# Dilated attention's merge: factors spread through DRAM, the sum of two groups on GpSimd, output weights loaded earlier

## The chip, the cores and the metric

The kernel runs on one core of a Trainium2 chip. The metric is the device time of one execution in microseconds (us); where several runs are given, their median stands for the kernel. The engines of a core run side by side, each in its own order: TensorE (PE; PEld is its weight load), VectorE (DVE), ScalarE (ACT), GpSimd (POOL), and SyncE (SP), which issues nearly all DMAs here. All arithmetic is in 32-bit floats. TensorE multiplies in a rounded 32-bit format (`F32R`), so every operand is split into a high and a low part, and a product is three matmuls (hi x hi, hi x lo, lo x hi).

## The reference

A trunk of two layers over 1024 positions of width 1024. Layer 0 is a gated MLP mixer, layer 1 dilated attention; each is followed by a dense MLP. The change lies in layer 1:

```python
for g, (window, dil) in enumerate(((128, 1), (512, 4), (2048, 16))):
    n_, d_, m_ = _dilated_group(...)     # numerator, denominator, row maximum of this group
...
m_all = jnp.max(jnp.stack(maxs), axis=0)
scales = [jnp.exp(m_ - m_all) for m_ in maxs]
num_sum = sum(n_ * c[..., None] for n_, c in zip(nums, scales))
den_sum = sum(d_ * c for d_, c in zip(dens, scales))
o = (num_sum / den_sum[..., None]).astype(h.dtype).reshape(B_, S_, ATT_WIDTH)
return o @ w_out
```

Each of 8 heads of width 64 attends in three groups of its own keys (dilations 1, 4 and 16). For each position and head the three results are added with three factors, which depend on the groups' maxima and denominators alone.

## The kernel before

Activations lie with features on the partitions and positions along the row. The attention stage works on 4 pairs of heads (`hp`), each pair in three units (`g` in the order 1, 2, 0), so 12 units. The main loop `unit_qkv(i)` computes the queries and keys of unit `i`, two products `m` of 48 matmuls of 128x512; the last unit has a third product for its values. While PE works on them, `attention()` fits in the scores, softmax and values of the unit before, in four steps `j`.

The order of PE's instructions is written out by a planner, `Flow`. It holds a clock that every matmul advances by an estimate. Side jobs are Python generators that yield a time after which they may go on (many from the table `LAT`, in ns), or an event and a time. Between the main loop's matmuls the planner lets those that are due put out their next instructions (`pump`); where the main loop has to wait for an event, `until` moves the clock to the next due side job. The other engines and SP's queue are ordered by a scheduler of the framework, by program order with a preference for what is marked `high_priority`, and as soon as operands and buffers are there. So loads are issued as far ahead as buffers allow.

The buffers that matter: `wpool`, tag "w", 8 tiles of 128x1024; a weight from `weight()` takes two of them (high and low part), loaded through 4 raw tiles (tag "r") and split at L208 (ScalarE, high part) and L209 (VectorE, low part). `at_bank()` gives one of 5 PSUM banks, `temp()` one of 8 tiles of 128x512.

`merge(hp, i)` (L1234) joins the three groups of one pair for one half `i` of the positions; there are 8 such calls. It begins when the last group's scores of that half are put out. It first forms the factors, `f`, with positions on the partitions: 128 x 3 groups x 4 blocks x 2 heads (L1242 to L1256). They are needed with features on the partitions. So for each group `factors(g)` copies the factors to 64 columns per head (L1262, ScalarE, 128x512) and `spread_factors` transposes the four 128x128 blocks into a PSUM bank (L187, PE). Then the group's numerator `N`, permuted back to the order of positions, is multiplied by it (L1279, VectorE); groups 1 and 2 are added up (L1283), and group 0's numerator is multiplied in place and gets that sum (L1290, L1291). `split_N` splits the result into the tiles `o`. For pairs 0 and 1 `project_side` follows, eight projections of `o` with the output weights `wbo` (`mm<-o`, three matmuls each, added to `h` at L306); pair 2's and 3's projections stand at the end of the stage. The next pair's values wait, in the plan, for the event `merged[hp, 1]`.

Other DMAs on SP's queue in this stage: the exchange of softmax statistics through DRAM (`sc<-st`, `ex<-sc`, L1223 to L1229), the bias tiles (`t<-bvec`, L906 and L911, copied by VectorE at L916) and the values (`V<-vd`).

Of the kernel before, what the change touches and what calls it, by code (L numbers as in the profile page):

```python
# [10 lines left out]
F32 = mybir.dt.float32  # L11
# [96 lines left out]

LAT = dict(sum=2600.0, rms=2600.0, tile=1600.0, gate=8500.0, soft=4200.0, turn=3800.0, fe=1300.0, v=2000.0, qk=2700.0, merge=2600.0, out=700.0, fex=3.0, ve=1600.0, vd=6000.0)


@with_exitstack
def trunk(ctx: ExitStack, tc: tile.TileContext, xT, w_u, w_v, w_o, w_s, b_s, w_qkv, w_vt, w_bo, rel,
# [910 lines left out]
    def unit_qkv(i):  # L1024
# [42 lines left out]
        if i < NU - 1:  # L1067
            flow.add(v_load(i))
        for m in range(3 if i == NU - 1 else 2):
            w = load(m)  # L1070
            if i == NU - 1 and m:
                proj_load(m + 1)
            both(w, KCOLS, ys, lambda s, b: out(m, s, b))
# [160 lines left out]
    def merge(hp, i):  # L1234
# [8 lines left out]
        nc.vector.tensor_tensor(mn, mn, e[2][:, :, :, 0], op=ALU.min)  # L1243
        f = small.tile([P, 3, 4, 2], F32, tag="f", name="f", bufs=2)
        for g in range(3):
            nc.vector.tensor_tensor(f[:, g], mn, e[g][:, :, :, 0], op=ALU.subtract)
        nc.scalar.activation(f, f, AF.Exp)
        dn = small.tile([P, 4, 2], F32, tag="dn", name="dn", bufs=2)
# [17 lines left out]
        def spread_factors(fe):  # L1266
            pb = at_bank()
            for b in range(4):
                transpose(pb[:, blk(b)], fe[:, blk(b)])
            return pb  # L1270

        rest = None
        fe_ns = LAT["fe"] * (2.2 if hp == 3 else LAT["fex"])
        for g in (1, 2):
            fe = factors(g)
            yield fe_ns
            pb = spread_factors(fe)
            t = temp()
            nc.vector.tensor_tensor(own(t, g), permuted(us_[g].N, i, g), own(pb, g), op=ALU.mult)  # L1279
            if rest is None:  # L1280
                rest = t
            else:
                nc.vector.tensor_tensor(rest, rest, t, op=ALU.add)  # L1283
        fe = factors(0)
        yield fe_ns
        yield valued[hp, i], 0
        N = us_[0].N[:, half(i)]
        pb = spread_factors(fe)
        with tc.high_priority(offset=PRIO):
# [39 lines left out]
    def project_side(hp, i):  # L1329
        for m in range(8 - LEFT * ((hp, i) == (1, 1))):  # L1330
            project(hp, i, m)
            yield 900
        projected[hp, i].t = flow.t
# [128 lines left out]
```

## Time and profile before

| What | Value |
|---|---|
| time before, median of 3 runs | 2188.39 us (2188.21 to 2189.08) |
| the profiled execution | 2188.09 us, span 2186.4 us |
| mean granted TensorE clock | 0.995 |
| PE, DVE, ACT, POOL busy | 2142.4, 1551.1, 1087.4, 515.5 us |
| attention stage with its merges | about 1085 to 1545 us of the span |

A row of a group reads: line, engine, operation, out<-in by tile names, shapes, count, then busy us and mean ns of one, then idle time of the engine just before and what ended it. A row of the timeline reads: start, length, engine, line, operation, count. A row of the stretches reads: stretch, length, busy us (and instructions) of PE, PEld, DVE, ACT, POOL, then clock, DMA share and GB/s. A row of the waits reads: who waited, for whom, us in total, times, longest.

### The profile page before, as it was taken

The page shows a single profiled execution, that of the slowest core. Times are in us where ns is not written, and L with a number is a line of the kernel's source. Part 1 is how long each engine was busy: PE and PEld are TensorE (multiplying, and loading weights), DVE is VectorE, ACT ScalarE, POOL GpSimd, SP SyncE. Part 2 cuts the span into 40 slices and gives each one's busy share as a digit, 9 for nine tenths or more (in the row PEclk, how much of TensorE's full clock was granted, in tenths as well). Part 3 has the DMA queues.
Part 4 walks back from the last instruction along what each step waited for, and adds up shares of the span by engine and source line. Part 5 has one row for each costly group of instructions (what it writes and reads, how often), then busy time and mean ns, then how long its engine had stood idle before and what let it go on. Part 6 is the DMA issues. An engine that isn't in the chain of part 4 may idle for free.

```text
span 2186.4 us, 30394 instructions
## 1 busy us (share of the span) xinstructions
PE 2142.4 (98%) x10360; PEld 1776.8 (81%) x10360; DVE 1551.1 (71%) x2855; ACT 1087.4 (50%) x2200; POOL 515.5 (24%) x372
## 2 busy tenths in 40 slices
PE   8999999999999999999999999999999999999997
PEld 7888887888878888788888887887778888788886
DVE  7875268766689887771357676658986667988867
ACT  7644135555564444351355564656555556544433
POOL 2000124333323333510000000001443332332335
PEclk9999999999999999999999999999999999999999
DMA  6321104444355443333322222221154443644422
GB/s 222 110 75 49 48 22 150 165 150 152 132 172 172 151 155 117 109 113 138 121 68 62 74 65 54 75 55 30 39 179 157 149 152 121 195 161 150 150 90 99
DMA packets 167679, 253.88 MB, mean 116 GB/s; under 512 B 33641, under 2 KB 59364, under 8 KB 167524
## 3 DMA queue, kind: packets, MB, share of 16 engines
q1 hardware_dynamic: 166768, 250.71, 35.7%
q8 instruction: 81, 1.33, 0.3%
q10 hardware_dynamic: 756, 1.23, 0.2%
q14 instruction: 74, 0.61, 0.1%
HBM read 182.50 MB, written 69.37 MB: 115 GB/s over the span
## 4 chain that ended last, share of the span: by engine, by line
PE 77%; DVE 10%; DMA 6%; ACT 4%; issue 2%; POOL 1%; SPq 1%; DVEq 0%; ACTq 0%; POOLq 0%
PE at L180 38%; PE mm L180 37%; PE at L187 1%; DVE wp L209 1%; ACT t L1107 1%; DMA t<-bvec 1%; DMA h<-in_xT 1%; DMA t<-hid 1%; DMA t<-in_w_dl 1%; DVE y L209 1%; DMA sc<-st 1%; DVE h L797 1%; DVE N L1145 1%; DMA hr<-hid 1%; DVE hx L209 1%
## 5 line engine op out<-in xcount | busy, mean ns | idle before, releaser
L208 ACT ACTIVATE wp<-r 128x512 fp32r<-128x512 f32 (+2 forms) x404 | 240.6, 600 | 359.1 <-PE at L180 240.3
L180 PE MATMUL at<-hx,wp 128*128 128x512 f32 x1770 | 413.1, 389 | 3.7 <-DVE h L797 3.7
L180 PE MATMUL mm<-y,whi 128*128 128x512 f32 x1312 | 412.3, 395 | 0.0
L180 PEld LDWEIGHTS at<-hx,wp 128*128 128x128 f32 x1770 | 332.0, 188 | 73.8 <-DVE h L797 4.5
L209 DVE TENSOR_TENSOR wp<-r,wp 128x512 fp32r<-128x512 f32 (+2 forms) x404 | 319.9, 801 | 66.0 <-ACT wp L208 62.3
L180 PE MATMUL at<-t,wp 128*128 128x512 f32 x1344 | 313.9, 389 | 0.1
L180 PEld LDWEIGHTS at<-t,wp 128*128 128x128 f32 x1344 | 252.2, 188 | 52.8 <-DVE t L713 0.5
L262 POOL TENSOR_TENSOR t<-t 128x512 f32<-128x512 f32 (+1 forms) x66 | 82.8, 1255 | 866.2 <-ACT t L257 864.1
L180 PEld LDWEIGHTS mm<-y,whi 128*128 128x128 f32 x1312 | 240.7, 188 | 50.6
L180 PE MATMUL mm<-y,wlo 128*128 128x512 f32 x656 | 255.9, 390 | 0.0
L180 PE MATMUL mm<-y,wp 128*128 128x512 f32 x912 | 224.3, 392 | 5.3 <-ACT t L694 4.8
L349 POOL TENSOR_TENSOR t<-r 128x512 f32<-128x512 f32 (+3 forms) x62 | 90.4, 1457 | 579.4 <-DMA r<-in_w_dn 164.2
L180 PEld LDWEIGHTS mm<-y,wp 128*128 128x128 f32 x912 | 171.5, 189 | 43.4 <-ACT t L694 5.7
L180 PE MATMUL mm<-hx,wp 128*128 128x512 f32 x708 | 172.4, 390 | 2.5 <-DVE hx L209 1.3
L180 PEld LDWEIGHTS mm<-hx,wp 128*128 128x128 f32 x708 | 132.6, 188 | 31.5 <-DVE hx L209 2.3
L209 DVE TENSOR_TENSOR hx<-t,hx 128x512 fp32r<-128x512 f32 x192 | 146.6, 770 | 1.8 <-ACT hx L208 1.8
L180 PEld LDWEIGHTS mm<-y,wlo 128*128 128x128 f32 x656 | 123.1, 188 | 26.6
L797 DVE TENSOR_TENSOR h<-h,at 128x512 f32<-128x512 f32 x144 | 97.6, 682 | 48.2 <-PE at L180 46.4
L209 DVE TENSOR_TENSOR wlo<-r,whi 128x512 fp32r<-128x512 f32 x138 | 97.6, 725 | 46.4 <-ACT whi L208 42.0
L208 ACT ACTIVATE hx<-t 128x512 fp32r<-128x512 f32 x192 | 119.0, 630 | 18.1 <-DMA t<-hid 11.7
L208 ACT ACTIVATE whi<-r 128x512 fp32r<-128x512 f32 x138 | 84.0, 627 | 88.3 <-PE mm L180 56.9
L180 PE MATMUL at<-y,wp 128*128 128x512 f32 x480 | 119.0, 390 | 0.7 <-DVE wp L209 0.7
(199 smaller groups left out, 3214.0 us busy)
## 6 DMA issues: line engine op xcount, KB each, us to landing
t<-hid SPq DMA_DIRECT2D x182, 256.0 KB, 3.5
hid<-t SPq DMA_DIRECT2D x140, 256.0 KB, 2.3
r<-in_w_up SPq DMA_DIRECT2D x128, 256.0 KB, 2.7
r<-in_w_dn SPq DMA_DIRECT2D x88, 256.0 KB, 2.6
hid<-b SPq DMA_DIRECT2D x56, 256.0 KB, 2.1
r<-in_w_qkv SPq DMA_DIRECT2D x50, 256.0 KB, 2.6
r<-in_w_v SPq DMA_DIRECT2D x48, 256.0 KB, 3.5
vd<-vs SPq DMA_DIRECT2D x16, 512.0 KB, 3.9
```

What stands on the lines that cost most here:

```text
L180: nc.tensor.matmul(out, lhsT, rhs, **kw)
L187: nc.tensor.transpose(out, src, ident)
L208: nc.scalar.activation(hi, src, AF.Copy)
L209: nc.vector.tensor_tensor(lo, src, hi.bitcast(F32), op=ALU.subtract)
L262: nc.gpsimd.tensor_tensor(self.acc, self.acc, sq, op=ALU.add)
L349: tt(r3, r[0, 0], r[1, 0], op=ALU.subtract)
L797: engine.tensor_tensor(hs[i, s], hs[i, s], src, op=ALU.add)
L1107: nc.scalar.activation(p[:, c], p[:, c], AF.Exp, bias=m, scale=-1.0, accum_out=dn)
L1145: nc.vector.tensor_tensor(o, o, pv[r, c], op=ALU.add)
```

## The change

For pairs 0, 1 and 2 the factors no longer go through ScalarE and PE. `f` is laid out so that its 24 columns (group, head, block) lie together. One transpose turns them into 24 rows of 128 (L187), VectorE copies these out of PSUM, and one DMA stores them in DRAM as 3 x 2 rows of 512 positions. Six DMAs read them back, each row to 64 partitions, into two tiles of `wpool`'s tag "w". All this is put out at once, after which the planner waits 11 us. The products of groups 1 and 2 and their sum are done by GpSimd, from SBUF; group 0's product stays on VectorE and reads SBUF instead of PSUM. Pair 3's two merges are as before. `proj_load(0)` and `proj_load(1)`, the output weights of pairs 0 and 1, are put out at the start of the first unit of the next pair instead of at the first projection. The planner leaves 1400 ns between two projections at the side, where it left 900.

```diff
@@ -106,7 +106,7 @@
 WARM = 11
 MMB = 3
 
-LAT = dict(sum=2600.0, rms=2600.0, tile=1600.0, gate=8500.0, soft=4200.0, turn=3800.0, fe=1300.0, v=2000.0, qk=2700.0, merge=2600.0, out=700.0, fex=3.0, ve=1600.0, vd=6000.0)
+LAT = dict(sum=2600.0, rms=2600.0, tile=1600.0, gate=8500.0, soft=4200.0, turn=3800.0, fe=1300.0, v=2000.0, qk=2700.0, merge=2600.0, out=700.0, sent=11000.0, proj=1400.0, ve=1600.0, vd=6000.0)
 
 
 @with_exitstack
@@ -1066,6 +1066,8 @@
 
         if i < NU - 1:
             flow.add(v_load(i))
+        if g == ORDER[0] and 0 < u.hp < 3:
+            proj_load(u.hp - 1)
         for m in range(3 if i == NU - 1 else 2):
             w = load(m)
             if i == NU - 1 and m:
@@ -1241,10 +1243,11 @@
         mn = small.tile([P, 4, 2], F32, tag="mn", name="mn", bufs=2)
         nc.vector.tensor_tensor(mn, e[0][:, :, :, 0], e[1][:, :, :, 0], op=ALU.min)
         nc.vector.tensor_tensor(mn, mn, e[2][:, :, :, 0], op=ALU.min)
-        f = small.tile([P, 3, 4, 2], F32, tag="f", name="f", bufs=2)
+        flat = small.tile([P, 3, 2, 4], F32, tag="f", name="f", bufs=2)
+        f = flat.rearrange("p g a b -> p g b a")
         for g in range(3):
             nc.vector.tensor_tensor(f[:, g], mn, e[g][:, :, :, 0], op=ALU.subtract)
-        nc.scalar.activation(f, f, AF.Exp)
+        nc.scalar.activation(flat, flat, AF.Exp)
         dn = small.tile([P, 4, 2], F32, tag="dn", name="dn", bufs=2)
         d2 = small.tile([P, 4, 2], F32, tag="d2", name="d2", bufs=2)
         nc.vector.tensor_tensor(dn, f[:, 0], e[0][:, :, :, 1], op=ALU.mult)
@@ -1269,23 +1272,49 @@
                 transpose(pb[:, blk(b)], fe[:, blk(b)])
             return pb
 
+        def sent():
+
+            pt = at_bank()
+            transpose(pt[0:24, 0:P], flat.rearrange("p g a b -> p (g a b)"))
+            ft = temp()[0:24, 0:P]
+            fd = dram.tile([3, 2, HALF], F32, tag="fd", name="fd")
+            with tc.high_priority(offset=PRIO):
+                nc.vector.tensor_copy(ft, pt[0:24, 0:P])
+                nc.sync.dma_start(fd.rearrange("g a (b p) -> (g a b) p", p=P), ft)
+            out = {}
+            place = [wpool.tile([P, 2, HALF], F32, tag="w", name="fe") for _ in range(2)]
+            for g in (1, 2, 0):
+                out[g] = place[g == 0][:, g // 2]
+                with tc.high_priority(offset=PRIO):
+                    for a in range(2):
+                        nc.sync.dma_start(out[g][64 * a:64 * a + 64], fd[g, a].partition_broadcast(64))
+            return out
+
         rest = None
-        fe_ns = LAT["fe"] * (2.2 if hp == 3 else LAT["fex"])
+        fe_ns = LAT["fe"] * 2.2
+        if hp < 3:
+            by_dma = sent()
+            yield LAT["sent"]
         for g in (1, 2):
-            fe = factors(g)
-            yield fe_ns
-            pb = spread_factors(fe)
+            if hp < 3:
+                pb = by_dma[g]
+            else:
+                fe = factors(g)
+                yield fe_ns
+                pb = spread_factors(fe)
             t = temp()
-            nc.vector.tensor_tensor(own(t, g), permuted(us_[g].N, i, g), own(pb, g), op=ALU.mult)
+            engine = nc.vector if hp == 3 else nc.gpsimd
+            engine.tensor_tensor(own(t, g), permuted(us_[g].N, i, g), own(pb, g), op=ALU.mult)
             if rest is None:
                 rest = t
             else:
-                nc.vector.tensor_tensor(rest, rest, t, op=ALU.add)
-        fe = factors(0)
-        yield fe_ns
+                engine.tensor_tensor(rest, rest, t, op=ALU.add)
+        if hp == 3:
+            fe = factors(0)
+            yield fe_ns
         yield valued[hp, i], 0
         N = us_[0].N[:, half(i)]
-        pb = spread_factors(fe)
+        pb = by_dma[0] if hp < 3 else spread_factors(fe)
         with tc.high_priority(offset=PRIO):
             nc.vector.tensor_tensor(N, N, pb, op=ALU.mult)
             nc.vector.tensor_tensor(N, N, rest, op=ALU.add)
@@ -1329,7 +1358,7 @@
     def project_side(hp, i):
         for m in range(8 - LEFT * ((hp, i) == (1, 1))):
             project(hp, i, m)
-            yield 900
+            yield LAT['proj']
         projected[hp, i].t = flow.t
 
     all_values()
```

## The prediction

> **What bounds the kernel now.** I read the page's busy times first, then one table of stretches over the attention stage (1085 to 1475 us), then the waits of that stage.
>
> ```profile
> span 2186.4 us, 30394 instructions
> PE 2142.4 (98%) x10360; PEld 1776.8 (81%) x10360; DVE 1551.1 (71%) x2855; ACT 1087.4 (50%) x2200; POOL 515.5 (24%) x372
> PE 77%; DVE 10%; DMA 6%; ACT 4%; issue 2%; POOL 1%; SPq 1%; DVEq 0%; ACTq 0%; POOLq 0%
> ```
>
> TensorE is busy for 98% of the span and carries 77% of the chain that ended last. The change lies in the attention stage only, so I look there. Columns: stretch, length, then busy us of PE, PEld, DVE, ACT, POOL.
>
> ```profile
> 1085.00:1162.00 77.00, 76.52 (x461) 62.72 (x460) 40.43 (x140) 42.42 (x131) 0.00 (x0) 1.00 0.26 69
> 1162.00:1182.00 20.00, 20.00 (x137) 17.39 (x136) 16.36 (x57) 15.23 (x40) 0.00 (x0) 1.00 0.25 80
> 1182.00:1277.00 95.00, 93.21 (x549) 76.86 (x548) 63.12 (x178) 49.57 (x145) 0.00 (x0) 1.00 0.23 63
> 1277.00:1297.00 20.00, 20.00 (x137) 17.40 (x136) 16.12 (x54) 14.42 (x37) 0.00 (x0) 1.00 0.25 79
> 1297.00:1390.00 93.00, 91.07 (x536) 74.32 (x535) 58.31 (x168) 47.13 (x140) 0.00 (x0) 1.00 0.23 59
> 1390.00:1411.00 21.00, 21.00 (x141) 18.21 (x140) 17.28 (x59) 16.21 (x42) 0.00 (x0) 1.00 0.24 77
> 1411.00:1475.00 64.00, 63.05 (x395) 52.71 (x393) 40.48 (x122) 37.65 (x112) 0.00 (x0) 1.00 0.23 56
> ```
>
> In these 390 us PE stands for 0.48 + 1.79 + 1.93 + 0.95 = 5.15 us in all. GpSimd does nothing. The three 20 us stretches are where the first merges of pairs 0, 1 and 2 begin: VectorE is at 16.4 of 20 us there, the only other engine near its limit. So PE work taken out here is time saved, as long as nothing new makes PE stand; at most 5.15 us of standing can be won on top.
>
> **What is removed.** Each of the six merges of pairs 0 to 2 (three pairs, two halves) spreads its factors three times, each time by one ScalarE copy (L1262) and four transposes (L187). Two of these spreads between matmuls:
>
> ```profile
> 1173.34 0.60 PE L187 MATMUL at<-ident,t 128*128 128x128 f32 x4
> ...
> 1186.27 0.66 PE L187 MATMUL at<-ident,t 128*128 128x128 f32 x4
> 1186.68 0.70 PE L180 MATMUL mm<-y,whi 128*128 128x512 f32 x2
> ...
> 1188.14 0.60 PE L187 MATMUL at<-ident,t 128*128 128x128 f32 x4
> 1188.50 0.71 PE L180 MATMUL mm<-y,whi 128*128 128x512 f32 x2
> ```
>
> Start to start, four transposes push the next matmul by 1186.68 - 1186.27 = 0.41 us, or 0.36. Eighteen spreads by 0.41 are 7.4 us of PE (6.5 by the other). Each merge adds one transpose, 0.10 us, so 0.6 comes back: 6.8 us net, 5.9 at the low end.
>
> ```profile
> DVE b L916 <- DMA t<-bvec: 26.2, 10, 4.6
> PE at L187 <- ACT t L1262: 0.6, 2, 0.3
> ```
>
> With the copies goes the 0.6 us that PE waited for them. Sum so far -7.4.
>
> VectorE and ScalarE are relieved too:
>
> ```profile
> L262 POOL TENSOR_TENSOR t<-t 128x512 f32<-128x512 f32 x54 | 74.0, 1371 | 860.4 <-ACT t L257 858.9
> L1279 DVE TENSOR_TENSOR t<-N,at 128x512 f32<-128x512 f32 x16 | 17.4, 1085 | 0.0
> L1262 ACT ACTIVATE t<-f 128x512 f32<-128x512 f32 x24 | 14.8, 621 | 3.2 <-DVE t L1283 3.2
> L1290 DVE TENSOR_TENSOR N<-N,at 128x512 f32<-128x512 f32 x8 | 5.5, 683 | 0.5 <-PE at L187 0.5
> L1283 DVE TENSOR_TENSOR t<-t 128x512 f32<-128x512 f32 x8 | 5.3, 668 | 0.1
> ```
>
> Per merge VectorE loses two products of 1.085 and one sum of 0.668, 2.84 us; ScalarE 3 x 0.621 = 1.86 us. Neither bounds the stage, so I book nothing for that; the bound on the gain side is the rest of PE's standing, 5.15 - 0.6 = 4.5 us. VectorE's new copy out of PSUM has 24 partitions; the 128-partition L1290 at 0.68 us bounds it from above, and VectorE's relief covers it.
>
> **What is added: the way of the factors.** I follow merge (0, 0). The planner placed group 1's old transposes 3.9 us after the factors were issued, so the new single transpose stands near 1173.34 - 3.9 = 1169.4. Then copy, store, and six loads on SP.
>
> ```profile
> hid<-t SPq DMA_DIRECT2D x140, 256.0 KB, 2.3
> t<-bvec SPq DMA_DIRECT2D x8, 256.0 KB, 4.1
> t<-bvec SPq DMA_DIRECT2D x8, 32.0 KB, 2.8
> sc<-st SPq DMA_DIRECT2D x8, 8.0 KB, 4.0
> ```
>
> A store lands in 2.3 us (wide rows) to 4.0 (16-byte pieces). The factors' rows are 512 bytes, so I take 2.3; either way, with at most 0.7 for the copy and 0.6 for an issue (below), the loads could go by 1169.4 + 0.7 + 0.6 + 4.0 = 1174.7. But they write into two tiles of the "w" pool, which has eight and which the weights fill as soon as a pair comes free:
>
> ```profile
> 1162.31 0.62 ACT L208 ACTIVATE whi<-r 128x512 fp32r<-128x512 f32 x1
> ...
> 1181.90 0.64 ACT L208 ACTIVATE whi<-r 128x512 fp32r<-128x512 f32 x1 [0.16 <-PE mm L180]
> ```
>
> Each row is a weight's split that starts when PE has done with an older weight (the second row says so). The pair that comes free at 1162.31 goes to a weight, since the factors are not there yet; the next at 1181.90. So the store is hidden, and the loads start at 1181.90.
>
> ```profile
> 1183.40 1.26 SPq L911 DMA_DIRECT2D t<-bvec  x2
> ```
>
> Two issues take 1.26 us, so group 1 lands at 1181.90 + 1.26 + 2.8 = 1186.0 (4.1 instead of 2.8 at the upper end), group 2 at 1187.2. On GpSimd no strided product is in the trace. Lower bound: L262's plain 1.37 us. Upper: the same product on VectorE takes 1.085 against 0.683 for a plain one, a factor of 1.59, which makes 2.18 us. I take 2.18, since L1279 has the same operands. So 1188.2, 1190.4, and with a sum of 1.37 1191.7. What follows is as before:
>
> ```profile
> 1189.77 0.69 DVE L1291 TENSOR_TENSOR N<-N,t 128x512 f32<-128x512 f32 x1
> 1190.50 0.64 ACT L208 ACTIVATE o<-N 128x512 fp32r<-128x512 f32 x1
> 1191.72 0.69 DVE L209 TENSOR_TENSOR o<-N,o 128x512 fp32r<-128x512 f32 x1
> 1193.86 0.70 PE L180 MATMUL mm<-o,whi 128*128 128x512 f32 x2
> ```
>
> Last sum, split: 1191.7 + 0.69 + 0.64 + 0.69 = 1193.7. Two spreads fewer before the release bring all of it forward by 0.8, to 1192.9. The planned first projection was at 1193.86; four spreads fewer ahead of it bring it to 1192.2. PE would stand 0.7 us. Lower bound 0 (with 1.37 the chain is 1.6 shorter); upper, with 4.1 per load, 2.0. Pairs 0 and 1 have this; pair 2 is projected only at the end, and second halves find the first half's tiles free and have to wait for its projection in any case. So 2 x 0.7 = 1.4 us, ends 0 and 4.0.
>
> The Trainium skill has a price for such a load in "DMA: Bandwidth & Descriptors", section "Anatomy of one DMA — SWDGE (gpsimd) path": about 2.0 us plus the bytes at 436 GB/s, for DMAs that GpSimd issues. As an estimate, 128 KB would land in 2.3 us, 0.5 sooner than the row that I used; by it the term would be 0.4 and the sum 1.0 us lower.
>
> **What is queued behind the new waits.** SP: behind the six loads stands the next bias tile (1183.40), 6 x 0.63 = 3.8 us later; its taker is VectorE's copy L916, which stands in VectorE's order. VectorE also stands at the products and sums of N until load and GpSimd are done. What such standing costs can be read off: VectorE stood 26.2 us for bias loads in 10 waits (2.6 each), and PE's standing apart from the copies was 4.5 us in all, so at most 0.17 us of PE per us of VectorE. Six merges at 2.6 are 15.7 us, at most 2.7 of PE; lower end 0. I take the middle, 1.3.
>
> **Output weights ahead.** Their loads, four DMAs and four splits for pairs 0 and 1, move past a unit's two weight loads on SP.
>
> ```profile
> 1117.04 0.89 SPq L169 DMA_DIRECT2D r<-in_w_bo  x2
> ```
>
> They are issued 77 us before first use already, being hoisted. Moved further they hold a pair of tiles longer, and two weights are split one step of the pool later (1181.90 - 1162.31 = 19.6 us). The pool's four pairs hold three weights beside the one that PE reads, so two steps of lead are left. Zero, covered by that lead; without it a first half's split, 0.64 + 0.69 us (the rows of o above), would stand ahead of each weight. **The projection's spacing** (900 to 1400 ns in the plan) costs zero too: PE has qkv matmuls to run between projections. Where it has none left, the planner moves its clock to the next due step, and the projections come back to back.
>
> **Sum.** -6.8 - 0.6 + 1.3 + 1.4 = -4.7 us. The profiled execution took 2188.1 us (span 2186.4 and 1.7 around it), the median of the runs is 2188.4. Forecast 2183.7. What a measurement of this kernel can tell from no change is about 0.2%, 4.4 us: faster begins under 2184.0.
>
> **Rivals.** (a) All of the way is hidden: pools and GpSimd idle, nothing stands; -7.4, 2181.0. For: GpSimd is free, ScalarE and PSUM banks are relieved. Against: tiles are claimed the moment they come free. (b) The freed PE time returns at the first projections and behind VectorE, both terms at their upper ends: -7.4 + 4.0 + 2.7 = -0.7, 2187.7, no change. For: the row of 1181.90. Against: it needs 4.1 us loads.
>
> (c) Slower: GpSimd's reads hold up VectorE, which then holds PE. GpSimd works 2 x 2.18 + 1.37 = 5.7 us per merge; if VectorE's work stood for all of it, it would lose 5.7 - 2.84 = 2.9 us per merge, six merges 17.2 us, all on PE where VectorE is the later one: -7.4 + 17.2 = +9.8, 2198. It turns slower once PE loses (7.4 + 4.4) / 6 = 2.0 us per merge.
>
> ```profile
> L209 DVE TENSOR_TENSOR wp<-r,wp 128x512 fp32r<-128x512 f32 x344 | 288.3, 848 | 61.1 <-ACT wp L208 57.6
> L209 DVE TENSOR_TENSOR wlo<-r,whi 128x512 fp32r<-128x512 f32 x138 | 97.6, 725 | 46.4 <-ACT whi L208 42.0
> ```
>
> For: the same subtraction takes 848 ns in the stage where GpSimd works and 725 where it mostly does not. Against: that is 17%, not a stop, and VectorE has 3.6 us of 20 free. The Trainium skill, "GPSIMD Engine Reference", section "1. Specifications", says that GpSimd shares its SBUF interfaces with VectorE, in contention with instructions that have two SBUF inputs. By that rule, taken as a full stop, this rival holds; the trace agrees in sign, with the 17%.
>
> **How the numbers follow.** Forecast 0.42, own range 2181.5 to 2186, three quarters of it (0.32) under 2184.0; (a) 0.20; (b) 0.16; (c) 0.22. Faster 0.32 + 0.20 = 0.52, same 0.10 + 0.16 = 0.26, slower 0.22. The range goes from 2179, (a) with 2 us of PE's other standing won, to 2195, which takes in (b) and the lower part of (c).
>
> **What would show it.** Right: about 66 fewer L187 transposes, PE busy some 7 us less, the first projections of pairs 0 and 1 waiting under 1 us for o, factor loads that start when a weight's matmuls end. (a): loads starting 3 us after the transpose. (b): PE standing 2 us at those projections. (c): VectorE's two-input rows stretched, and PE waiting for VectorE at scores and q, k. Wrong altogether: weights split too late for their matmuls, which I priced at nothing.

## The result, and the profile after

The changed kernel takes 2200.98 us (median of six runs, 2196.49 to 2202.48); the kernel before took 2188.73 in six runs beside it (2187.60 to 2190.91). The ratio is 1.0053, 95% interval 1.0040 to 1.0066: 12.3 us slower. The forecast of 2183.7 has the wrong sign, and the time lies above the range.

The profiled execution is the quickest of the six, 2196.49 us. Its page, two of the rows that the prediction showed of before:

```profile
span 2194.6 us, 30326 instructions
PE 2140.8 (98%) x10294; PEld 1770.3 (81%) x10294; DVE 1549.0 (71%) x2843; ACT 1078.0 (49%) x2182; POOL 545.7 (25%) x390
```

PE has 66 instructions fewer, as forecast (10360 to 10294), but only 1.6 us less busy time, and the span is 8.2 us longer. The table of stretches, with the prediction's borders (busy us of PE, PEld, DVE, ACT, POOL, then the clock):

```profile
1085.00:1162.00 77.00, 76.88 (x469) 63.65 (x467) 39.63 (x142) 42.40 (x132) 0.00 (x0) 1.00 0.24 63
1162.00:1182.00 20.00, 19.80 (x128) 16.62 (x127) 15.64 (x42) 11.22 (x31) 4.48 (x3) 1.00 0.37 120
1182.00:1277.00 95.00, 88.78 (x512) 71.48 (x513) 59.09 (x167) 46.37 (x135) 5.08 (x4) 1.00 0.27 71
1277.00:1297.00 20.00, 20.00 (x130) 17.10 (x129) 15.84 (x59) 13.12 (x37) 0.18 (x1) 1.00 0.25 73
1297.00:1390.00 93.00, 88.72 (x510) 71.42 (x510) 57.28 (x164) 45.13 (x133) 9.31 (x6) 1.00 0.30 78
1390.00:1411.00 21.00, 21.00 (x141) 17.91 (x140) 16.46 (x57) 14.14 (x40) 0.05 (x1) 1.00 0.22 68
1411.00:1475.00 64.00, 60.11 (x349) 48.85 (x348) 42.18 (x121) 35.76 (x102) 9.17 (x6) 0.97 0.32 92
```

In these 390 us PE stood 5.15 us before; now it stands 14.7. Before, the clock was 1.00 in every stretch; now the last shows 0.97. Whom PE waits for, from 1110 to 1500 us (total, times, longest):

```profile
PE at L187 <- DVE f L1259: 4.7, 3, 1.9
PE at L187 <- ACT t L1109: 3.5, 13, 0.6
PE at L180 <- DVE tr L209: 2.4, 5, 0.9
PE mm L180 <- DVE h L306: 1.9, 4, 0.8
```

The first row is new: the single transpose of the factors waits for VectorE's last product L1259 (L1256 before). The others are VectorE's and ScalarE's usual products arriving late; the second was 2.3 us before (row in the section on why the prediction was wrong).

For comparing runs I use one measure below. The **stage** goes from the first exchange store (`sc<-st`) to the last pair of them: 1110.7 to 1473.6 us before, 362.9 us; 371.4 us after, 8.45 longer. Summed from start to start over PE's instructions, transposes (L187) take 7.2 us less than before (40.7 to 33.5), so the term for the removed work had its size. But the same 1038 matmuls `mm` take 10.7 us more (246.8 to 257.5) and the 252 value products (128x128) 3.0 more: that is where waits and half clock sit.

The half clock shows only in narrow stretches. Here are two neighbouring ones of the changed kernel, and then, in the same view for L187 alone (busy us of PE and PEld), the transposes' part of the first:

```profile
1442.34:1445.76 3.42, 2.52 (x19) 1.65 (x20) 1.88 (x9) 3.31 (x12) 0.00 (x0) 1.00 0.00 1
1445.76:1449.17 3.41, 3.41 (x9) 2.63 (x9) 3.11 (x11) 2.80 (x9) 0.00 (x0) 0.50 0.51 150
```

```profile
1442.34:1445.76 3.42, 1.48 (x6) 0.68 (x6) 1.00 0.00 1
```

In the first, PE is busy for 2.52 of 3.42 us, but 1.48 of that are transposes; matmuls take 1.04 us, 30%. In the next the granted clock is 0.50, which costs up to half of 3.41 us. Before had none between 1085 and 1500 us. The granted clock of whole runs points the same way: the ten runs of before in one session had 0.9948 in the mean, the five of the changed kernel beside them 0.9912. As (1 - clock) x time that is 11.4 against 19.4 us, so up to 8 us of the 12.3 are clock ("up to", since part of it lies over waits).

### The profile page after: what moved, and what is told of

The parts are those of the page before. It is cut to its first block, busy times and chain, and to the rows that moved or that the text cites. A ratio compares the mean times of both kernels' runs of the same rounds, so it can differ in the third digit from the quotient of the medians.

```text
span 2194.6 us, 30326 instructions
## 1 busy us (share of the span) xinstructions
PE 2140.8 (98%) x10294; PEld 1770.3 (81%) x10294; DVE 1549.0 (71%) x2843; ACT 1078.0 (49%) x2182; POOL 545.7 (25%) x390
## 4 chain that ended last, share of the span: by engine, by line
PE 78%; DVE 10%; DMA 4%; ACT 4%; issue 2%; POOL 1%; SPq 1%; DVEq 0%; ACTq 0%; POOLq 0%
PE at L180 40%; PE mm L180 37%; DVE wp L209 1%; ACT t L1109 1%; PE at L187 1%; DMA fe<-fd 1%; DMA sc<-st 1%; DMA t<-bvec 1%; DVE y L209 1%; DVE h L306 1%; DVE hx L209 1%; DVE N L1147 1%; DVE h L797 1%; SPq L1290 0%; DVE t L209 0%
## 5 line engine op out<-in xcount | busy, mean ns | idle before, releaser
L208 ACT ACTIVATE wp<-r 128x512 fp32r<-128x512 f32 (+2 forms) x404 | 241.0, 600 | 366.6 <-PE at L180 247.4
L1307 POOL TENSOR_TENSOR t<-N,fe 128x512 f32<-128x512 f32 x12 | 20.5, 1732 | 464.4 <-PE at L180 426.1
L208 ACT ACTIVATE whi<-r 128x512 fp32r<-128x512 f32 x138 | 83.3, 625 | 97.0 <-PE mm L180 56.5
L208 ACT ACTIVATE hx<-t 128x512 fp32r<-128x512 f32 x192 | 118.8, 630 | 14.3 <-DMA t<-hid 10.1
```

Of the source, the lines that this page charges most:

```text
L208: nc.scalar.activation(hi, src, AF.Copy)
L1307: engine.tensor_tensor(own(t, g), permuted(us_[g].N, i, g), own(pb, g), op=ALU.mult)
```

## The experiments

All times are medians of five rounds against the kernel before on the same chip. "Stage" is the change against before's 362.9 us, "stands" what PE stands in it (pauses over 0.15 us), "half clock" half the time at 0.50 in it, all from the profiled run.

| Kernel | us | ratio to before, 95% interval | stage | stands | half clock |
|---|---|---|---|---|---|
| before | 2186.8 to 2188.7 | | 0 | 4.9 | 0 |
| c1_changed_again | 2200.99 | 1.0053 [1.0039, 1.0066] | +13.3 | 14.4 | 6.8 |
| e1_vector_sum | 2196.18 | 1.0045 [1.0032, 1.0059] | +8.6 | 11.7 | 6.8 |
| e2_later_transpose | 2211.24 | 1.0110 [1.0096, 1.0124] | +21.9 | 18.1 | 15.4 |
| e3_plan_only | 2191.57 | 1.0017 [1.0008, 1.0026] | 0.0 | 4.8 | 0 |
| e4_temps | 2211.40 | 1.0110 [1.0096, 1.0123] | +22.4 | 24.5 | 10.2 |
| g1_same_plan_vector | 2195.89 | 1.0040 [1.0027, 1.0054] | +6.7 | 14.1 | 3.4 |
| g2_same_plan_pool | 2196.36 | 1.0039 [1.0027, 1.0050] | +6.1 | 13.0 | 3.4 |
| g3_spacing_back | 2200.23 | 1.0054 [1.0042, 1.0066] | +9.2 | 15.3 | 6.8 |
| h1_hold | 2188.81 | 1.0005 [0.9996, 1.0014] | -2.1 | 4.9 | 0 |
| h2_hold_one | 2190.72 | 1.0011 [1.0002, 1.0020] | +0.8 | 6.8 | 0 |
| h3_own_tiles | 2249.27 | 1.0277 [1.0263, 1.0291] | +10.7 | 15.2 | 6.8 |
| h3c_fewer_temps | 2252.03 | 1.0293 [1.0279, 1.0307] | +15.4 | 15.1 | 12.0 |
| k1_pool_queue | 2213.77 | 1.0116 [1.0102, 1.0130] | +24.8 | 20.2 | 18.8 |
| k2_store_alone | 2189.40 | 1.0007 [0.9999, 1.0016] | -0.7 | 4.3 | 0 |
| k3_after_pool_queue | 2214.30 | 1.0117 [1.0102, 1.0133] | +25.6 | 27.0 | 15.4 |
| k4_inplace | 2214.22 | 1.0115 [1.0101, 1.0129] | +24.0 | 25.4 | 18.8 |
| m1_no_spreads | 2203.74 | 1.0069 [1.0055, 1.0083] | +13.5 | 14.8 | 12.0 |
| m2_idle_spreads | 2198.19 | 1.0047 [1.0035, 1.0060] | +8.3 | 9.0 | 1.7 |

No version beat the kernel before.

### Parts of the changed kernel

The first theories: GpSimd stretches VectorE (A); the factors' tiles in the weights' pool and the output weights ahead delay the weights (B); the single transpose stands too early in PE's order (C).

**The changed kernel again:** 

> The changed kernel unaltered, on the same chip as the three others: 2197 to 2203, granted clock 0.990 to 0.994.

It repeats, at 12.4 us more than before.

**Sums on VectorE:**

```diff
-            engine = nc.vector if hp == 3 else nc.gpsimd
+            engine = nc.vector
```

> The changed kernel, but the products of groups 1 and 2 and their sum are VectorE's again in all eight merges; the way through DRAM, the tiles and the plan stay. Theory A (while GpSimd reads, VectorE's two-input instructions are stretched: group 0's product 1.91 us instead of 0.69, a small subtraction 1.52 instead of 0.16, and PE then waits for VectorE): the stretching goes, PE's standing of 9.5 us more falls to under 3, the time to 2184 to 2190 (before 2188.7, changed 2201.0). Theory B (the pool's tiles and the output weights moved ahead cost the time): no change from the changed kernel, 2198 to 2202. Theory C (the single transpose is planned too early for the factors to be there): VectorE has 2.84 us more to do per merge, so PE's waits of 1.94, 1.16 and 1.57 us at the second halves' transposes stay at half or more: 2193 to 2198.

PE's waits, to be set against those of the changed kernel:

```profile
PE at L187 <- ACT t L1109: 4.8, 18, 0.6
PE mm L180 <- DVE h L306: 3.4, 5, 1.2
```

The wait for `f` (4.7 us) is gone, so GpSimd made it. But the median falls by 4.8 us only, with intervals that overlap, and 8 us of loss stay: other waits grow. The changed kernel's timeline at GpSimd's first two products, with the rows of POOL, DVE and PE that meet there:

```profile
1177.44 3.50 POOL L1307 TENSOR_TENSOR t<-N,fe 128x512 f32<-128x512 f32 x2 [237.35 <-PE at L180]
...
1177.62 1.91 DVE L1319 TENSOR_TENSOR N<-N,fe 128x512 f32<-128x512 f32 x1 [0.58 <-DMA fe<-fd]
1179.45 1.52 DVE L1249 TENSOR_TENSOR f<-mn,st 128x8 f32<-128x8 f32 x1
...
1183.74 0.27 PE L187 MATMUL at<-ident,f 128*24 128x128 f32 x1 [1.94 <-DVE f L1259]
```

VectorE's product L1319 takes 1.91 us where L1290 took 0.68 before, and a subtraction of 128x8 takes 1.52 (0.17 before, see the last section). The first begins while GpSimd's products run, and the second ends at 1180.97, 0.03 us after them (1177.44 + 3.50 = 1180.94). With the sums on VectorE the same two operations take 0.69 and 0.17 us in the mean, with the same operands, so it is GpSimd that stretches them. The second half's factors come late by that, and PE stands 1.94 us for them.

**Transposing later** (the single transpose 3.9 us later in the plan, where the first spread stood) and **factors in temporaries** instead of the weights' pool:

```diff
+            yield 3900.0
             by_dma = sent()
-            yield LAT["sent"]
+            yield LAT["sent"] - 3900.0
```

```diff
-            place = [wpool.tile([P, 2, HALF], F32, tag="w", name="fe") for _ in range(2)]
...
-                out[g] = place[g == 0][:, g // 2]
+                out[g] = temp()
```

> The changed kernel with the planner's pause before the single transpose lengthened by 3900 ns and the pause after it shortened by as much. Theory C: the 4.7 us that PE waits for the factors at the three second halves go, and with them what follows from it: 2193 to 2197. Theory A: these waits go too, but VectorE is held as long, so PE's other waits (for q and k, for the sums into h) stay and part of the gain comes back there: 2196 to 2200. Theory B: no change, 2199 to 2202.

> The changed kernel, with the spread factors in three tiles of the temporaries' pool per merge instead of two tiles of the weights' pool. Theory B: the weights are split ahead as far as before, and the time falls to 2186 to 2193. Theory A and C: the weights' lead was enough in any case; within 2 us of the changed kernel, 2199 to 2203.

Both are some 23 us slower than before, 10 us slower than the changed kernel. With the transpose later, PE no longer waits for `f`, but 7.8 us for two sums of `h` (4.6 the longest), and nine stretches of half clock follow. With temporaries, PE waits 7.5 us for `o` in two waits. So C falls as a remedy, and the weights' pool was the better place for the factors.

**Plan only** (output weights ahead and 1400 ns of spacing put into the kernel before), and **the reverse**, both taken out of the changed kernel:

```diff
+        if g == ORDER[0] and 0 < u.hp < 3:
+            proj_load(u.hp - 1)
...
-            yield 900
+            yield 1400.0
```

> The kernel before, with only two parts of the change: the output weights of pairs 0 and 1 loaded at the start of the next pair's first unit, and 1400 ns between projections at the side. No way through DRAM, no GpSimd. Theory B: most of the loss is here, 2194 to 2201. Theories A and C: as before within 2 us, 2187 to 2191.

> The changed kernel with 900 ns between projections again and the output weights of pairs 0 and 1 loaded at the first projection. If these two parts carry the new order's loss: 2193 to 2198. If the single pause of 11 us and GpSimd carry it: 2199 to 2203.

Put in, they cost 3.7 us with nothing lost inside the profiled stage; taken out, nothing is won (1.0054 against 1.0053).

### The plan of before, with the way through DRAM

Two more theories: PE's new order is at fault (P), or the way through DRAM itself (D). Here PE's order is that of before, the spreads missing and the single transposes added; the output weights are loaded at the first projection.

```diff
         if hp < 3:
             by_dma = sent()
-            yield LAT["sent"]
+            flow.t -= TRANSPOSE
         for g in (1, 2):
             if hp < 3:
+                yield 3900.0
+                flow.pe(4 * TRANSPOSE)
                 pb = by_dma[g]
```

In the first the sums are VectorE's, in the second GpSimd's:

> The factors of pairs 0 to 2 through DRAM as in the change, but products and sums on VectorE, and the planner keeps the pauses of the kernel before: three of 3900 ns per merge, its clock moved on by the transposes that are no longer there, 900 ns between projections, output weights loaded at the first projection. Theory P (the loss without GpSimd is the new order of PE's work: qkv matmuls are used up sooner and thin work is left to stand by itself, where the granted clock halves too): with the old order the 6.8 us of transposes are won and little else is lost, 2180 to 2186. Theory D (the way through DRAM itself is late: loads, tiles of the weights' pool, the single transpose waiting for the factors): the loss stays, 2192 to 2198. Before is 2187.9, the changed kernel 2201.0.

> The same as the kernel with the old plan and VectorE's sums, but products of groups 1 and 2 and their sum on GpSimd as in the change. Theory A (GpSimd stretches VectorE's instructions, PE then waits at the second halves' transposes): 4 to 8 us above that kernel. If GpSimd's reads hurt only in the new plan: within 2 us of it.

Still 7 to 8 us slower, with either engine: P and A together stand for 5 of the 12.3 us and are not the main cause, and GpSimd's price hangs on the plan (0.5 us here, 4.8 between e1 and the changed kernel).

### Single suspects in the kernel before

Three things that the way through DRAM brings, each alone: two tiles of the weights' pool held through a merge, one tile, and a store on SP's queue that stands until the factors are there. Theory B' says that the weights lose their lead.

```diff
+        held = [wpool.tile([P, 2, HALF], F32, tag="w", name="held") for _ in range(2 if hp < 3 else 0)]
+        for x in held:
+            nc.gpsimd.tensor_copy(x[:, 0, 0:8].rearrange("p (a b) -> p a b", b=2), f[:, 0])
...
+        for x in held:
+            nc.gpsimd.tensor_tensor(x[:, 0, 0:8], x[:, 0, 0:8], N[:, 0:8], op=ALU.add)
```

```diff
+        if hp < 3:
+            fd = dram.tile([P, 3, 4, 2], F32, tag="fd", name="fd")
+            with tc.high_priority(offset=PRIO):
+                nc.sync.dma_start(fd, f)
```

> The kernel before, with all its spreads on TensorE and its plan; two tiles of the weights' pool are taken at each merge of pairs 0 to 2 (GpSimd writes eight columns of them from the factors) and given back after the sum (GpSimd adds N's first eight columns). Theory B' (the two tiles take the weights' lead, weights are split late and bunched, TensorE stands): the stage of three merges grows by 8 to 15 us, TensorE stands 13 to 16 us in it instead of 4.9, the time is 2197 to 2204. Theory D (the way through DRAM itself, its loads or its single transpose): no tile is loaded here, so the time stays within 2 us of before, 2187 to 2191.

> As h1_hold with one tile of the weights' pool instead of two. Theory B': between before and h1_hold, 2190 to 2197. Theory D: 2187 to 2191.

> The kernel before with one thing more: in each half of the first three pairs SP stores the factors (128x24 values) to DRAM, ahead of what it has queued, and nobody reads them. No tile of the pools is held, TensorE does all its spreads. Theory Q: TensorE stands 10 to 15 us in the stage instead of 4.9; 2193 to 2200. Theory T: within 2 us of before, 2185 to 2190.

Next to nothing: 1.0005, 1.0011 and 1.0007. B' falls for the tiles held by themselves. The splits of weights (ScalarE, L208) show why it had looked good. The changed kernel first, then the kernel that only holds tiles:

```profile
1129.89 0.62 ACT L208 ACTIVATE whi<-r 128x512 fp32r<-128x512 f32 x1
1172.08 1.14 ACT L208 ACTIVATE whi<-r 128x512 fp32r<-128x512 f32 x2
1190.47 1.15 ACT L208 ACTIVATE whi<-r 128x512 fp32r<-128x512 f32 x2
```

```profile
1161.60 1.15 ACT L208 ACTIVATE whi<-r 128x512 fp32r<-128x512 f32 x2
...
1190.10 1.13 ACT L208 ACTIVATE whi<-r 128x512 fp32r<-128x512 f32 x2
```

The changed kernel splits no weight for 42 us. Holding two tiles alone does the same (none in the 45 us up to 1161.60) and bunches splits, so the kept tiles are the likely reason, but PE stands no longer than before: there the lead suffices, as the prediction had it. One thing differs. h1's bunch at 1190.10 comes after the softmax's exponentials of that place (the last begins at 1189.61); in the kernels with the way through DRAM it comes ahead of them, as the rows of m2 below show. That case h1 does not test.

### Tiles, queue and temporaries

**Tiles of their own** for the factors, at the price of two temporaries, and the price alone:

```diff
-    tpool = ctx.enter_context(tc.tile_pool(name="tpool", bufs=8))
+    tpool = ctx.enter_context(tc.tile_pool(name="tpool", bufs=6))
...
-                out[g] = place[g == 0][:, g // 2]
+                out[g] = tpool.tile([P, HALF], F32, tag="fe", name="fe", bufs=2)
```

> The kernel of g1_same_plan_vector (plan of before, factors through DRAM, all sums on VectorE) with the factors in two tiles of their own and the temporaries cut from eight to six, so that the weights' pool is untouched. Theory B': TensorE stands 5 to 9 us in the stage instead of 14.1, and the 66 transposes saved show: 2182 to 2189. Theory D: as g1_same_plan_vector, 2194 to 2198. If six temporaries are too few, the waits for ScalarE's and VectorE's temporaries grow, here and in h3c_fewer_temps alike.

> g1_same_plan_vector with six temporaries instead of eight and nothing else: what h3_own_tiles pays for its memory. Theory B' and theory D both: g1_same_plan_vector's 2195.9 plus the price of two temporaries, an estimate of 0 to 5 us: 2195 to 2201.

Inconclusive: two temporaries fewer cost 56 us, 23 of them ahead of the stage, where one wait of 17.9 us stands that before does not have. Giving the weights' pool back wins 2.8 us of that. Besides, these are two tiles of 128x512 for three factors, so the third also has to wait for a tile.

**GpSimd's queue instead of SP's** for the store and the loads, with the plan of before (k1), in the changed kernel (k3), and with no temporaries in these merges (k4, products in the factors' place). Theory Q says that SP's queue stands, T that temporaries lack.

```diff
-                nc.sync.dma_start(fd.rearrange("g a (b p) -> (g a b) p", p=P), ft)
+                nc.gpsimd.dma_start(fd.rearrange("g a (b p) -> (g a b) p", p=P), ft)
...
-                        nc.sync.dma_start(out[g][64 * a:64 * a + 64], fd[g, a].partition_broadcast(64))
+                        nc.gpsimd.dma_start(out[g][64 * a:64 * a + 64], fd[g, a].partition_broadcast(64))
```

> The kernel of g1_same_plan_vector (plan of before, factors through DRAM, sums on VectorE) with the factors' store and six loads of each half issued by GpSimd, which has nothing else to do there, instead of SP. Theory Q (SP stands at the store until the factors are there, with the weights' loads queued behind, which then land late and are split in a bunch): the loads of the query and key weights go at their old times (two near 1165 us instead of 1175.9, the next before 1185 instead of 1190.8), TensorE stands 4 to 8 us in the stage instead of 14.1, 2183 to 2189. Theory T (temporaries held longer): as g1_same_plan_vector, 2194 to 2198.

> The changed kernel with the factors' store and loads issued by GpSimd, ahead of the sums that it forms. Theory Q: the changed kernel's 2201.0 less what SP's standing costs, 8 to 12 us, to 2189 to 2193, with the waits for the factors at the single transposes (about 5 us) left. Theory T: 2198 to 2203.

> k1_pool_queue without temporaries in the first three pairs' merges: the transposed factors pass through the unused half of the second tile, and the products are formed in the factors' place. Theory Q: k1_pool_queue's time or up to 2 us less. Theory T: 5 to 10 us less than k1_pool_queue.

k1 is 17.9 us slower than g1, k3 13.3 slower than the changed kernel, and k4 no quicker than k1, so T falls. Q falls by the store alone (k2, 1.0007), and because the weights' loads still go at 1174.97 and 1195.57 in k1, with SP free of the factors. What made k1 slower is another thing; VectorE's and PE's rows show it:

```profile
1180.96 1.03 DVE L1307 TENSOR_TENSOR t<-N,fe 128x512 f32<-128x512 f32 x1 [5.97 <-DMA fe<-fd]
...
1185.00 0.27 PE L187 MATMUL at<-ident,f 128*24 128x128 f32 x1 [4.60 <-DVE f L1257]
```

VectorE stands 5.97 us for the loads, the second half's factors are queued behind on it, and PE stands 4.60 at their transpose. On SP's queue, in g1, the same stand (L1307, fe) comes to 2.0 us in the whole stage.

### The spreads themselves

Left over were two accounts. F: the spreads lay under waits that PE would have had anyway. L: they were worth their 7 us, and the way through DRAM costs some 14 by itself. So: take the spreads out of the kernel before without the way through DRAM (m1; the factors are then multiplied untransposed, so its result is not the attention's), and put spreads that nobody reads beside it (m2).

```diff
         def spread_factors(fe):
+            if hp < 3:
+                flow.pe(4 * TRANSPOSE)
+                return fe
             pb = at_bank()
```

```diff
+        def idle_spread():
+            pb = at_bank()
+            for b in range(4):
+                transpose(pb[:, blk(b)], ident)
...
-                flow.pe(4 * TRANSPOSE)
+                idle_spread()
```

> The kernel before with the 72 spreads of the first three pairs' merges left out: VectorE multiplies with the factors as ScalarE copied them, untransposed (so this part of the computation is not done). Plan, order, tiles and queues are those of before; there is no way through DRAM. Theory F: TensorE stands 9 to 13 us in the stage instead of 4.9, with up to two stretches at half clock; 2185 to 2191. Theory L: TensorE stands as before, 2179 to 2183.

> The kernel of g1_same_plan_vector (plan of before, way through DRAM, sums on VectorE) with TensorE transposing the identity twelve times in each half at the places of the old spreads; nobody reads the results. Theory F: TensorE stands 5 to 9 us in the stage instead of 14.1, no stretch at half clock, and the time is that of g1_same_plan_vector or less in spite of the added work: 2190 to 2196. Theory L: the added work counts in full, 2200 to 2206.

Taking 72 transposes out, with nothing added, makes the kernel 15.6 us slower: further than F expected, and against L. Some two thirds of that turn out to be the doing of this edit alone (below). The two largest of PE's waits in m1:

```profile
PE at L187 <- ACT t L1107: 6.1, 15, 0.7
PE mm L180 <- ACT o L208: 4.2, 2, 2.1
```

The place where it begins, PE in m1 (four rows), then in the kernel before (three), then the first of the four exponentials there, in before and in m1:

```profile
1190.52 0.33 PE L187 MATMUL at<-ident,t 128*128 128x128 f32 x1 [0.50 <-ACT t L1107]
1191.02 0.71 PE L187 MATMUL at<-ident,t 128*128 128x128 f32 x3 [0.17 <-ACT t L1107]
1192.41 0.44 PE L187 MATMUL at<-ident,t 128*128 128x128 f32 x2 [0.68 <-ACT t L1107]
1192.78 1.08 PE L180 MATMUL at<-k,q 64*128 64x128 f32 x12
```

```profile
1191.34 0.60 PE L187 MATMUL at<-ident,t 128*128 128x128 f32 x4
1192.19 0.44 PE L187 MATMUL at<-ident,t 128*128 128x128 f32 x2 [0.24 <-ACT t L1107]
1192.56 0.96 PE L180 MATMUL at<-k,q 64*128 64x128 f32 x12
```

```profile
1188.80 0.40 ACT L1107 ACTIVATE t<-t,st 128x128 f32<-128x128 f32 x1 [0.88 <-DVE st L1105]
```

```profile
1189.97 0.40 ACT L1107 ACTIVATE t<-t,st 128x128 f32<-128x128 f32 x1 [1.29 <-DVE st L1105]
```

PE comes to the softmax's transposes 0.8 us earlier, since spreads ahead of them are gone. ScalarE's exponentials are not earlier; the first begins 1.2 us later, because VectorE now does the last product, the last sum and the split of `o` ahead of the softmax's steps instead of between and after them, and the fourth ends 0.2 us later (1192.26 against 1192.04). So PE waits three times, 1.35 us in all, and the next scores begin at 1192.78, 0.2 us later than before. VectorE's new order explains these 0.2 us, not the loss of the 0.8: in the kernel before, too, PE waited for the fourth exponential (0.24 us, the row at 1192.19), so the scores would not have begun before 1192.56 however early PE came. The stretch of that place and the one after, m1 first with the transposes' part of the first stretch in a fence of its own, then before likewise:

```profile
1190.04:1193.45 3.41, 2.08 (x16) 1.35 (x18) 1.82 (x8) 3.41 (x11) 0.00 (x0) 1.00 0.00 0
1193.45:1196.87 3.42, 3.42 (x13) 2.59 (x10) 3.42 (x12) 1.75 (x8) 0.00 (x0) 0.50 0.00 0
```

```profile
1190.04:1193.45 3.41, 1.48 (x6) 0.68 (x6) 1.00 0.00 0
```

```profile
1190.04:1193.45 3.41, 3.17 (x26) 2.33 (x24) 2.71 (x6) 3.30 (x9) 0.00 (x0) 1.00 0.00 0
1193.45:1196.87 3.42, 3.42 (x19) 2.91 (x18) 3.42 (x12) 1.75 (x8) 0.00 (x0) 1.00 0.02 5
```

```profile
1190.04:1193.45 3.41, 1.05 (x7) 0.71 (x7) 1.00 0.00 0
```

Matmuls fill 0.60 us of m1's stretch (18%), 2.12 of before's (62%). In the next one m1's PE runs at 0.50 with 13 instructions where before put through 19. Over the stage, m1 has 9.8 us more of standing and 12.0 of half clock; with the stage 13.5 us longer, that leaves 8.3 us for PE's work saved.

How much of this belongs to the spreads? Set beside before matmul by matmul, m1's PE is level ahead of the first merge (0.03 us behind at before's 1170.18), 1.48 us ahead at 1190.88, 1.00 behind at 1195.09 and 0.37 behind at 1211.97: what four spreads had won is lost again at the place shown. Then, within 5 us, it falls to 5.3 behind. This second loss is not the spreads'. With them gone, the scheduler also placed one copy of the factors late, behind PE (ScalarE's row), and PE waits for the `o` that comes of it (PE's row):

```profile
1212.55 0.63 ACT L1262 ACTIVATE t<-f 128x512 f32<-128x512 f32 x1 [7.68 <-PE at L180]
```

```profile
1216.63 0.50 PE L180 MATMUL mm<-o,whi 128*128 128x512 f32 x1 [2.09 <-ACT o L208]
```

Pair 1 repeats both: from 5.29 us behind to 7.58 at its place of this kind, and to 12.98 with its late copy; pair 2, which has no projection at the side, ends at 14.29. So the two late copies, with the half clock after them, stand for some 10.3 us (4.9 and 5.4), and the rest for some 4: an estimate of what leaving out the spreads costs by itself, where the prediction had a gain of 7.4.

m2, the other way round, adds 7.4 us of transposes to g1 (18 x 0.41) and is 2.3 us slower, with intervals that overlap; PE stands 9.0 us instead of 14.1, and 1.7 us instead of 3.4 go to half clock. So two thirds of the added work lay under waits. But it is still 10.1 us slower than before with the same PE work: the way through DRAM costs something by itself. Of its 8.3 us in the stage, 4.0 are standing, 1.7 half clock; the other 2.6 (0.6 of them the six added transposes) I have not found.

Part of the standing can be followed in m2 at the same place, first on VectorE, then on ScalarE:

```profile
1188.00 0.29 DVE L916 COPY b<-t 128x256 f32<-128x256 f32 x1 [1.32 <-DMA t<-bvec]
...
1190.32 0.69 DVE L209 TENSOR_TENSOR wlo<-r,whi 128x512 fp32r<-128x512 f32 x1 [0.23 <-ACT whi L208]
```

```profile
1189.65 2.19 ACT L208 ACTIVATE whi<-r 128x512 fp32r<-128x512 f32 x4
1191.75 0.39 ACT L1107 ACTIVATE t<-t,st 128x128 f32<-128x128 f32 x1
```

The bias tile comes 1.1 us later than before (there L916 stands at 1186.89), VectorE then splits `o` and a weight ahead of the softmax's steps, and ScalarE four weights in a row ahead of the exponentials. The first of these begins at 1191.75, 2.95 us later than before; PE waits 0.66 us for it, and a stretch of half clock begins at 1194.69. So the late, bunched splits that cost nothing in h1 do stand in the softmax's way here; what share of the 10.1 us is theirs no run measured.

## Why the prediction was wrong

**The step that failed** is the sentence behind the table of stretches: "So PE work taken out here is time saved, as long as nothing new makes PE stand." Both halves of it failed. Forecast and measurement are 17.0 us apart (-4.7 and +12.3), and the runs, each against the kernel before beside it, split that into three:

| Part | booked | measured |
|---|---|---|
| the way through DRAM, PE's transposing work kept (m2) | +2.7 | +10.1 |
| the spreads left out beside it (m2 to g1) | -7.4 | -2.8, intervals overlap |
| GpSimd and the new plan (g1 to the changed kernel) | 0 | +5.0 |

The booked 2.7 are the terms 1.4 and 1.3; the single transposes (0.6) and the copies' waits (-0.6) cancel. Something new did make PE stand, far more than booked. And work taken out was not time saved: beside the way through DRAM it won 2.8 us, not clear of noise, and in m1 nothing. The size of the removed work was right (6.8 us booked with the single transposes, 7.2 measured in the changed kernel's stage), but in the merges PE is not alone in setting the pace: softmax, `q`, `k` and `h` reach it just in time from VectorE and ScalarE. The trace of before had it in one row:

```profile
PE at L187 <- ACT t L1107: 2.3, 12, 0.3
```

Twelve waits, none above 0.3 us, are not "standing that can be won". They say that PE runs at the heels of another chain in twelve places, and the spreads stood among them as filler. I read only the sum.

**The clock** had no term at all. Before shows 1.00 in all seven stretches, and I took that for given. In the changed kernel it is up to 8 of the 12.3 us, in m1 14.4 of the 15.4 us (means of the runs, by (1 - clock) x time), though 13.7 of the 23.9 us that m1's profiled stage spends at half clock lie behind its late copies.

**Loads waiting for a weight's tiles, +1.4:** wrong in its place. The framework keeps the tiles for the factors, and the loads go as soon as the store has landed, not at 1181.90:

```profile
1168.34 0.33 SPq L1283 DMA_DIRECT2D fd<-t  x1
1169.73 3.69 SPq L1290 DMA_DIRECT2D fe<-fd  x6
...
1189.69 0.63 PE L180 MATMUL mm<-o,whi 128*128 128x512 f32 x2
```

That is rival (a)'s sign, loads soon after the transpose; the first projection runs unhindered at 1189.69, where I had it waiting until 1192.9. The loads landed in 3.4 us (median of 36), where 2.8 was booked and the estimate beside it had 2.3. The term was 0, and the time was lost all the same.

**VectorE standing, +1.3:** the amount was too large and the price too small. VectorE stands 7.6 us for the factors' loads (four waits at L1319) and 0.8 us more than before for bias tiles, where 15.7 were booked. But I took 0.17 us of PE per us of VectorE from the mean over the stage. k1 shows another price at one place: 5.97 us of VectorE cost 4.60 of PE, since a later step of the same chain, the second half's factors, stands behind the wait.

**Slack that I did not see moved:** the second half's single transpose stands 3.9 us earlier in the plan than its old first spread; the prediction used that only for the store's date. With GpSimd stretching VectorE this became the 4.7 us at L1259.

**Rival (c)**, GpSimd holding up VectorE, came nearest in time (2198) and right in mechanism, and the rule of the Trainium skill, "GPSIMD Engine Reference", "1. Specifications", on shared SBUF interfaces is borne out by the rows of 1.91 and 1.52 us. But it explains the 4.7 us at L1259 and no more; without GpSimd 8 us remain. "17%, not a stop" was a mean over the dense stages; the rows show a stop (last section).

**Output weights and spacing, 0:** 3.7 us as a pair in the kernel before, nothing in the changed one. **Weights split too late**, "wrong altogether": the splits were late. Holding the tiles alone costs nothing, but in m2 they stand ahead of the softmax, not of the matmuls that need them; their price there is open.

**Open:** why the way through DRAM costs 10.1 us; the late exponentials of m2 are one piece of it. And the parts don't add up: alone the spreads left out cost some 4 us (m1 without its late copies, an estimate) and the way 10.1 (m2), together 7.3 (g1). Each shift of PE's work also moves which stretches fall to half clock, which may be the reason; no run shows it.

## What to carry to other kernels

An engine at 98% is no proof that its work can be taken out at a gain: look for many short waits of it on one producer, and ask what it would do in the time set free. Work can be cover: taking it out won next to nothing here while the chain beside it (softmax) stayed as late as it was. A run that only deletes something is not clean for that: lay it beside the old one instruction by instruction, since the scheduler moves other work into the gap, as m1's late copies show. Where PE's matmuls are thin, look at the granted clock in narrow stretches, and cost a stand of PE with the slow stretch that may follow, not by its own length alone.

## What the runs showed of the hardware

Half clock comes in stretches of 3.41 us on a fixed grid within a run. In 18 traces (all but h3 and h3c) 41 such runs of stretches begin in the stage. Each begins right after a stretch in which matmuls other than transposes took at most half of the time, in 28 of them more than 20%. Of the some 1850 other stretches at full clock that stayed at full clock, 33 were that thin, 19 of them with transposes filling PE to about 80%. So a thin stretch stood ahead of every half clock here, but only 41 of 74 thin ones were followed by it. The Trainium skill, "TensorE: Matmul & The Clock Gate", Part 1, has the free-running window of 3413 ns and the half clock after an idle window; the traces agree on the length, 3.41 us, but here no idle window was needed: 18% of matmuls (m1, 1190.04) or 30% (the changed kernel, 1442.34) sufficed.

GpSimd's products with two SBUF inputs did not slow VectorE's operations with two SBUF inputs by a share, they stopped them: eight of the 128x8 ones took 0.91 to 1.52 us in the changed kernel's stage, and each of the eight ended 0.02 to 0.03 us after an operation of GpSimd. Over the stage L1319 took 1232 ns in the mean and the 128x8 subtractions 624; without GpSimd (e1) the same two take 687 and 169. The trace of before has 683 for L1290 (shown in the prediction) and this:

```profile
1177.81 0.17 DVE L1246 TENSOR_TENSOR f<-mn,st 128x8 f32<-128x8 f32 x1
```

```profile
L1307 POOL TENSOR_TENSOR t<-N,fe 128x512 f32<-128x512 f32 x12 | 20.5, 1732 | 464.4 <-PE at L180 426.1 <-DMA fe<-fd 38.3
L1319 DVE TENSOR_TENSOR N<-N,fe 128x512 f32<-128x512 f32 x6 | 7.4, 1232 | 7.6 <-DMA fe<-fd 7.6
L1249 DVE TENSOR_TENSOR f<-mn,st 128x8 f32<-128x8 f32 x6 | 3.7, 624 | 0.1
```

The strided product itself takes GpSimd 1.73 us; I had taken 2.18.
